# Where the low half of a split weight unit comes from: a VectorE subtraction, or a ScalarE copy and an adding transfer

## The chip, the core and the metric

The kernel runs on one core of a Trainium2 chip. The metric is the device time of one execution in microseconds (us). TensorE (PE) does the matrix products, VectorE (DVE) and ScalarE (ACT) the elementwise work, GpSimd (POOL) a few small operations, and SyncE (SP) issues the loads and stores.

## What is computed

Two layers over 512 tokens of width 1024. Each layer normalises x, projects it to 8192 columns, mixes them by a gated short convolution and by retention over eight heads, and projects back:

```python
for layer in range(DEPTH):                      # DEPTH = 2
    h = rms_norm(x, pre_norm[layer])
    proj = jnp.einsum("bsd,dp->bsp", h, w_in[layer])          # 1024 -> 8192
    ...
    y_conv = c_b * causal_depthwise_conv(c_c * c_x, conv_w[layer])
    y_conv = y_conv * jax.nn.silu(c_z)
    ...
    ret = retention_chunkwise(q, k, v, log_gamma)             # chunks of 128
    ...
    mix = jnp.concatenate([y_conv.astype(h.dtype), y_ret], axis=-1)
    out = jnp.einsum("bse,ed->bsd", mix, w_out[layer])        # 2048 -> 1024
    x = x + rms_norm(out, post_norm[layer]).astype(x.dtype)
```

## The kernel before

The weights stream in as 168 units of 128 partitions x 2 x 512 float32 (512 KB each): 64 of w_in and 24 of w_out in layer 0, then 64 and 16 in layer 1. A unit is a slice of 256 rows of the product's inner dimension. Each product of float32 runs as three passes over operands split in two (hi + lo), so each unit is split once: ScalarE copies it to `wh`, rounded to a shorter significand (line 99), and VectorE subtracts, `wl = raw - wh` (line 100). A unit then feeds 24 matmuls: four targets x two halves x three passes (`mm3`, lines 252 to 254; L252 is hi x hi, and of the other two one takes `wl`).

`raw`, `wh` and `wl` have three buffers each, so unit i takes the buffers of unit i - 3. `prepare` splits units ahead of use, at most to the unit two past the one that PE works on, and `fetch` loads `raw` up to three units past that from SP's queue. So the split of unit i begins when PE has used unit i - 3 for the last time, and has to end before PE comes to unit i.

PE takes the units in groups of four: two together, target by target (`JOINT`), then two singly. A pair of heads takes four such groups, 16 units: the columns v and z (units 0 to 3 of the pair, with the activations as the stationary operand), q and k (4 to 7), and two convolution groups (8 to 11 and 12 to 15), in which the retention's own matmuls stand between the steps. w_out follows each layer. In layer 0 its second half of columns is done in two passes of two targets each, so units 72 to 87 feed only 12 matmuls each; the first units of layer 1 follow right behind.

In a group, the second unit (it takes the buffers of the single unit before) and the fourth (it takes those of the group's first unit) have the shortest time between the release of their buffers and PE's need. Units are counted from 0 here: unit 23 is the last of a q and k group, 25 and 29 are second units of the two convolution groups behind it, 33 the second and 35 the last of the next v and z group.

The framework orders the instructions of each engine by itself; an engine takes its own in order. VectorE also transposes the retention's result (`finish`, line 415), which ScalarE then splits (`mTh<-yT`). GpSimd runs the powers for the norms (lines 231, 396 and 466) and a small memset per convolution (line 427).

Of the kernel before, what the change touches and what calls it, by code (L numbers as in the profile page):

```python
# [12 lines left out]
AF = mybir.ActivationFunctionType  # L13
# [8 lines left out]
NKP = NK // 2  # L22
# [9 lines left out]


def _two_pi_parts():
    """2 * pi in parts (Cody and Waite); n * part is exact for all but the last."""
    rest = 2.0 * np.pi
    parts = []
    for bits in (8, 8, 8):
        e = np.floor(np.log2(abs(rest)))
        q = 2.0 ** (e - bits + 1)  # L40
        part = np.trunc(rest / q) * q
        parts.append(float(part))
        rest -= part
    parts.append(float(np.float32(rest)))
    return parts


# 10000 ** (-i / 64), i < 64, in float32
INV_FREQ = "0000803fd7af5d3f11f93f3fe03d263f9af50f3fcf53f93e9be8d73e1bf8ba3e9be8a13e04358c3e23d4723eed47523e8718363e40b01d3e778d083ed67fec3dcdcccc3d7859b13d0d94993d4dfe843dc255663d3f76473d15ba2c3d4893153de386013dd254e03c4f43c23c8b39a83c39ad913c334d7c3cf27b5a3c11333d3c0ad7233c2de10d3cb0b9f53b15cad43b9c44b83bcc919f3b772e8a3b0e526f3b383e4f3b0f77333b0d691b3b6f94063b2815e93a5cd7c93a8ec9ae3a0e5c973a6f12833ae201633a8c94443a443b2a3a166a133aac4fff392517dd39d774bf3960cba53972928f3915a87839e453573953773a391679213972d40b39e22cf238"

# column offsets in the table of constants
C_INVF = 0
C_MASK = C_INVF + 1
C_ID = C_MASK + P
# [20 lines left out]

@with_exitstack
def hybrid_trunk(ctx: ExitStack, tc, x, x_t, positions, pre_g, post_g, w_in, w_out, conv_w, consts, out):
    """Two layers on one core.

    Every product of a weight runs as three float32r passes over operands split  # L80
    exactly in two (hi + lo). The projection takes h without its factor
    r = rsqrt(mean(x^2) + eps) per token; r is applied behind it. The decays of the
    retention and r are scales of v and of the eps of the head norm.
    """
    nc = tc.nc
    PSUM = bass.MemoryType.PSUM

# [7 lines left out]
    aux = ctx.enter_context(tc.tile_pool(name="aux", bufs=3, space=PSUM))  # L95

    def split(dst_h, dst_l, src):
        """dst_h + dst_l = src, each of 12 significant bits."""
        nc.scalar.activation(out=dst_h, in_=src, func=AF.Copy)  # L99
        nc.vector.tensor_tensor(out=dst_l, in0=src, in1=dst_h.bitcast(F32), op=ALU.subtract)  # L100

# [3 lines left out]
            out=dst_l, in0=src, scalar=scale, in1=dst_h.bitcast(F32), op0=ALU.mult, op1=ALU.subtract  # L105
        )

# [1 line left out]
    units = []  # L109
    for l in range(DEPTH):  # L110
        units += [w_in[l, g, kp] for g in range(NG) for kp in range(NKP)]
# [17 lines left out]
    def prepare(n):  # L129
        while len(ws) <= min(n, len(units) - 1):  # L130
            i = len(ws)
            fetch(i)
            wh = wpool.tile([P, 2, 512], F32R, name=f"wh{i}", tag="wh")
            wl = wpool.tile([P, 2, 512], F32R, name=f"wl{i}", tag="wl")
            if i < NKP:
                for kk in range(2):
                    k = 2 * i + kk
                    split_scaled(hTh0[:, k, :], hTl0[:, k, :], xTs[i][:, kk, :], pre_c[:, 0, k : k + 1])
                    if i == 0:
                        split(wh[:, kk, :], wl[:, kk, :], raws[i][:, kk, :])  # L140
            if i:
                split(wh, wl, raws[i])
            ws[i] = (wh, wl)
            fetch(i + 3)

# [1 line left out]
    warm = cpool.tile([P, 1], F32, name="warm")  # L147
    nc.vector.memset(warm, 0.0)
    nc.scalar.activation(out=warm, in_=warm, func=AF.Silu)
# [5 lines left out]
    hTl0 = hpool.tile([P, NK, SEQ], F32R, name="hTl0", tag="hTl")  # L155
    fetch(2)

    # keeps TensorE's clock up until the first operands are there
    zero = tpool.tile([P, D], BF16, name="zero", tag="junk")
    nc.vector.memset(zero[:, :512], 0.0)  # L160
    pz = aux.tile([P, 512], F32, name="pz", tag="aux")
# [28 lines left out]
    def rotary_tables():  # L190
        ang = tpool.tile([P, SEQ], F32, name="ang", tag="sz")
        nn = tpool.tile([P, SEQ], F32, name="nn", tag="acc")
        nc.vector.tensor_copy(out=nn, in_=pos_i)
        nc.vector.tensor_scalar(
            out=ang, in0=nn, scalar1=cst[:, C_INVF : C_INVF + 1], scalar2=None, op0=ALU.mult
        )
        big = 1.5 * 2.0**23
        nc.vector.tensor_scalar(
            out=nn, in0=ang, scalar1=float(1.0 / (2.0 * np.pi)), scalar2=big, op0=ALU.mult, op1=ALU.add
        )  # L200
        nc.vector.tensor_scalar(out=nn, in0=nn, scalar1=big, scalar2=None, op0=ALU.subtract)
        for part in _two_pi_parts():
            nc.vector.scalar_tensor_tensor(
                out=ang, in0=nn, scalar=-part, in1=ang, op0=ALU.mult, op1=ALU.add
            )
        pi = 3.1415925
        nc.vector.tensor_scalar(out=ang, in0=ang, scalar1=pi, scalar2=-pi, op0=ALU.min, op1=ALU.max)
        nc.scalar.activation(out=sin_t, in_=ang, func=AF.Sin)
        # cos(r) = sin(pi/2 - |r|)
        nc.scalar.activation(out=ang, in_=ang, func=AF.Abs)  # L210
        nc.vector.tensor_scalar(
            out=ang, in0=ang, scalar1=-1.0, scalar2=float(np.pi / 2), op0=ALU.mult, op1=ALU.add
        )
        nc.scalar.activation(out=cos_t, in_=ang, func=AF.Sin)

# [1 line left out]
    def square_sum(l, t):  # L217
        junk = tpool.tile([P, D], BF16, name=f"jx_{l}_{t}", tag="junk", bufs=1)
        sq = nc.scalar.activation(out=junk, in_=xt[t], func=AF.Square, accum_out=sx[l][:, t : t + 1])  # L219
# [1 line left out]
            tc.keep_in_program_order(sq)  # L221

    def token_factors(l):
        """r, v's scale and the head norm's eps, for all tokens."""
        vx = rpool.tile([P, NT], F32, name=f"vx{l}", tag="vx", bufs=1)
        rx = rpool.tile([P, NT], F32, name=f"rx{l}", tag="rx", bufs=1)
        r2 = rpool.tile([P, NT], F32, name=f"r2{l}", tag="r2", bufs=1)
        vt = rpool.tile([P, NT, HEADS], F32, name=f"vt{l}", tag="vt", bufs=1)
        et = rpool.tile([P, NT, HEADS], F32, name=f"et{l}", tag="et", bufs=1)
        nc.vector.tensor_scalar(out=vx, in0=sx[l], scalar1=1.0 / D, scalar2=EPS, op0=ALU.mult, op1=ALU.add)  # L230
        nc.gpsimd.tensor_tensor(out=rx, in0=vx, in1=mhalf[:, :NT], op=ALU.pow)
        nc.vector.tensor_tensor(out=r2, in0=rx, in1=rx, op=ALU.mult)
        nc.vector.tensor_tensor(out=vt, in0=vtab, in1=r2.unsqueeze(2).to_broadcast([P, NT, HEADS]), op=ALU.mult)
        nc.vector.tensor_tensor(out=et, in0=etab, in1=vx.unsqueeze(2).to_broadcast([P, NT, HEADS]), op=ALU.mult)
        return rx, vt, et

    def factor_rows(l, rx):
        """r and r^2 of the tokens along the free dimension, on every partition."""
        rb = tpool.tile([P, NT, P], F32, name=f"rb{l}", tag="u", bufs=1, padded_shape=[P, NT, P + 1])
        nc.vector.tensor_copy(out=rb, in_=rx.unsqueeze(2).to_broadcast([P, NT, P]))  # L240
        ps = aux.tile([P, SEQ], F32, name=f"psr{l}", tag="aux")
# [5 lines left out]
        nc.scalar.activation(out=row2, in_=ps, func=AF.Square)  # L247
        return row, row2

# [1 line left out]
    def mm3(ps, ah, al, bh, bl, first, last):  # L251
        nc.tensor.matmul(out=ps, lhsT=ah, rhs=bh, start=first, stop=False)  # L252
        nc.tensor.matmul(out=ps, lhsT=ah, rhs=bl, start=False, stop=False)  # L253
# [2 lines left out]
    cursor = [0]  # L256

    def run_units(steps, targets, operands, hooks=None):
        """ps[t] += sum over the units. A step names units and targets (None: all) and takes
        the units target by target; hooks[i] are traced behind step i."""  # L260
        base = cursor[0]
        n = 1 + max(u for us, _ in steps for u in us)
        ps = {t: mm.tile([P, 512], F32, name=f"mm{base}_{t}", tag="mm") for t in targets}
# [27 lines left out]
            return wh[:, s], wl[:, s], ah[:, k, :], al[:, k, :]  # L291
        return operands

# [1 line left out]
    def take_vz(l, p, ps, rx, vt):  # L295
        vs, zs = [], []
        for t in range(NT):
# [29 lines left out]
    class Retention:  # L327
# [18 lines left out]
            self.sT.append(s)  # L346

        def k_natural(self, a):
            """Columns 32a : 32a + 32 of k, tokens on partitions."""
            if a == 0:  # L350
                self.kn = rpool.tile([P, 2, NT - 1, P], F32, name=f"kn_{self.tag}", tag="kn", bufs=1)
            src = self.kT.rearrange("p h (t j) -> p h t j", j=P)
            rows = slice(32 * a, 32 * a + 32)
            for b in range(4):
                cols = slice(32 * b, 32 * b + 32)
                nc.vector.transpose(out=self.kn[cols, :, :, rows], in_=src[rows, :, : NT - 1, cols])  # L356
# [49 lines left out]
                    )  # L406

        def finish(self, a):
            """Columns 32a : 32a + 32 of y, transposed; with the last of them, its parts."""
            if a == 0:  # L410
                self.yT = rpool.tile([P, 2, NT, P], F32, name=f"yT_{self.tag}", tag="yT", bufs=1)
            rows = slice(32 * a, 32 * a + 32)
# [4 lines left out]
                e = slice(4 * self.p, 4 * self.p + 2)  # L417
                split(self.mTh[:, e, :], self.mTl[:, e, :], self.yT.rearrange("p h t d -> p h (t d)"))

# [1 line left out]
    def conv(l, ct, ps, row, row2, mTh, mTl):  # L421
        pc, px, pz, pb = ps
        cc = tpool.tile([P, SEQ], F32, name=f"cc_{l}_{ct}", tag="cc")
# [20 lines left out]
        e = 4 * (ct // 2) + 2 + ct % 2  # L444
        split(mTh[:, e, :], mTl[:, e, :], acc)

# [1 line left out]
    def first_half(l, t, ps, og, post):  # L448
        """Columns 0 : 512 of an output row times the gain, and their part of its mean square + eps."""
        ss = rpool.tile([P, 1], F32, name=f"s0_{l}_{t}", tag="s0", bufs=4)  # L450
        v0 = rpool.tile([P, 1], F32, name=f"v0_{l}_{t}", tag="v0", bufs=4)
        junk = tpool.tile([P, 512], BF16, name=f"j0_{l}_{t}", tag="junk", padded_shape=[P, D])
# [34 lines left out]
            split(hTh[:, ks, s], hTl[:, ks, s], xg)  # L487
        return emit

# [1 line left out]
    hTh, hTl = hTh0, hTl0  # L491
    fac = {}

# [88 lines left out]


def _packed(x, positions, pre_norm, w_in, conv_w, w_out, post_norm):
    """The inputs laid out as the kernel reads them."""
    col = lambda kind, i: np.arange(kind * 1024 + i * P, kind * 1024 + (i + 1) * P)
    groups = []
    for p in range(NPAIR):
# [49 lines left out]
```

## Time and profile before

| | |
|---|---|
| time, median of 3 runs | 942.76 us (942.73 to 943.03) |
| profiled execution: span from the first to the last instruction | 941.0 us |
| median less that span | 1.8 us |
| PE busy | 933.1 us, 99% |
| DVE busy | 596.7 us, 63% |
| ACT busy | 278.4 us, 30% |
| POOL busy | 24.6 us, 3% |
| mean DMA rate | 103 GB/s |

The busy time of an engine is that of its instructions, waits left out. Matmuls overlap one another in the records, so a busy PE says that it had work, not that it ran at its peak. The timed runs carry no profile of their own; the profile is of one execution with the span above.

### The profile page before, as it was taken

To read this page: it belongs to the slowest core of one execution; us is meant where nothing else is said; L and a number is where in the kernel's file an instruction comes from. 1 tells how busy PE (TensorE), PEld (TensorE's weight loads), DVE (VectorE), ACT (ScalarE), POOL (GpSimd) and SP (SyncE) were. 2 spreads that over 40 slices of the span, in tenths; PEclk is the share of its full clock that TensorE was granted. 3 is DMA by queue.
4 is the path that set the end of the run, shared out by engine and by line. 5 is a ranking of instruction groups with operands and counts; after the bars stand their busy time and mean duration, and the time that the engine had idled before them with its cause. 6 is when DMAs were issued, how large, how long until landed. Compare 5 with 4: busy or idle time off the path is not lost.

```text
span 941.0 us, 10986 instructions
## 1 busy us (share of the span) xinstructions
PE 933.1 (99%) x4338; PEld 776.0 (82%) x4338; DVE 596.7 (63%) x960; ACT 278.4 (30%) x450; POOL 24.6 (3%) x46
## 2 busy tenths in 40 slices
PE   9999999999999999999999999999999999999997
PEld 6788888888888888888888888888888888888886
DVE  5595839583958395825764948394849484947324
ACT  5522331222133213324542133213321332222311
POOL 0000000000000000000000000000000000000000
PEclk9999999999999999999999999999999999999999
DMA  8522132213222322235532222322222222222222
GB/s 309 178 92 90 53 127 90 90 63 116 90 90 68 112 90 90 71 108 179 178 122 103 91 90 79 100 90 90 88 92 90 90 90 90 90 91 90 89 68 90
DMA packets 27700, 96.60 MB, mean 103 GB/s; under 512 B 3328, under 2 KB 3456, under 8 KB 27648
## 3 DMA queue, kind: packets, MB, share of 16 engines
q1 hardware_dynamic: 27504, 95.88, 30.7%
q8 instruction: 34, 0.56, 0.2%
q14 instruction: 18, 0.15, 0.1%
q10 hardware_dynamic: 144, 0.01, 0.0%
HBM read 93.78 MB, written 2.10 MB: 102 GB/s over the span
## 4 chain that ended last, share of the span: by engine, by line
PE 94%; DMA 2%; DVE 1%; ACT 1%; issue 1%; POOL 0%; SPq 0%; DVEq 0%; POOLq 0%; ACTq 0%
PE mm L252 30%; PE mm L254 29%; PE mm L253 29%; PE pa L378 2%; PE pss L339 2%; PE pa L382 1%; PE pk L361 1%; DMA xT<-in_x_t 1%; DMA x<-in_x 1%; DVE wl L100 1%; DMA pre_c<-in_pre_norm 0%; DVE x L470 0%; PE psx L481 0%; ACT wh L99 0%; ACT jx L219 0%
## 5 line engine op out<-in xcount | busy, mean ns | idle before, releaser
L100 DVE TENSOR_TENSOR wl<-raw,wh 128x1024 fp32r<-128x1024 f32 (+1 forms) x169 | 205.4, 1217 | 226.5 <-ACT wh L99 222.8
L99 ACT ACTIVATE wh<-raw 128x1024 fp32r<-128x1024 f32 (+1 forms) x169 | 178.1, 1054 | 470.6 <-PE mm L253 303.1
L252 PE MATMUL mm<-hTh,wh 128*128 128x512 f32 x768 | 302.5, 394 | 0.1
L254 PE MATMUL mm<-hTh,wl 128*128 128x512 f32 x768 | 299.8, 390 | 0.3 <-DVE wl L100 0.3
L253 PE MATMUL mm<-hTl,wh 128*128 128x512 f32 x768 | 298.7, 389 | 0.0
L254 PEld LDWEIGHTS mm<-hTh,wl 128*128 128x128 f32 x768 | 144.1, 188 | 31.4 <-DVE wl L100 0.7
L252 PEld LDWEIGHTS mm<-hTh,wh 128*128 128x128 f32 x768 | 144.3, 188 | 29.3 <-ACT z L304 0.6
L253 PEld LDWEIGHTS mm<-hTl,wh 128*128 128x128 f32 x768 | 144.3, 188 | 29.1
L252 PE MATMUL mm<-wh,hTh 128*128 128x512 f32 x256 | 99.6, 392 | 0.3 <-ACT hTh L99 0.3
L253 PE MATMUL mm<-wl,hTh 128*128 128x512 f32 x256 | 99.8, 390 | 0.0
L254 PE MATMUL mm<-wh,hTl 128*128 128x512 f32 x256 | 99.8, 390 | 0.0
L252 PE MATMUL mm<-wh,mTh 128*128 128x512 f32 x256 | 99.8, 390 | 0.0
L254 PE MATMUL mm<-wh,mTl 128*128 128x512 f32 x256 | 99.6, 389 | 0.0
L253 PE MATMUL mm<-wl,mTh 128*128 128x512 f32 x256 | 99.6, 389 | 0.0
L252 PEld LDWEIGHTS mm<-wh,hTh 128*128 128x128 f32 x256 | 48.1, 189 | 11.5 <-ACT wh L99 1.2
L415 DVE STREAM_TRANSPOSE yT<-y 32x256 f32<-32x256 f32 x128 | 55.8, 436 | 2.1
L253 PEld LDWEIGHTS mm<-wl,hTh 128*128 128x128 f32 x256 | 48.1, 188 | 10.5 <-DVE wl L100 0.6
L254 PEld LDWEIGHTS mm<-wh,mTl 128*128 128x128 f32 x256 | 48.0, 188 | 10.1
L254 PEld LDWEIGHTS mm<-wh,hTl 128*128 128x128 f32 x256 | 48.1, 188 | 9.9
L252 PEld LDWEIGHTS mm<-wh,mTh 128*128 128x128 f32 x256 | 48.1, 188 | 9.9
L253 PEld LDWEIGHTS mm<-wl,mTh 128*128 128x128 f32 x256 | 48.1, 188 | 9.9
L356 DVE STREAM_TRANSPOSE kn<-qk 32x192 f32<-32x192 f32 x128 | 47.3, 370 | 2.0
(85 smaller groups left out, 596.3 us busy)
## 6 DMA issues: line engine op xcount, KB each, us to landing
raw<-in_w_in SPq DMA_DIRECT2D x127, 512.0 KB, 3.3
raw<-in_w_out SPq DMA_DIRECT2D x40, 512.0 KB, 3.3
x<-in_x SPq DMA_DIRECT2D x4, 512.0 KB, 7.2
out<-x SPq DMA_DIRECT2D x8, 256.0 KB, 2.1
xT<-in_x_t SPq DMA_DIRECT2D x3, 512.0 KB, 7.7
post<-in_post_norm SPq DMA_DIRECT2D x2, 512.0 KB, 5.5
xT<-in_x_t SPq DMA_DIRECT2D x2, 256.0 KB, 3.9
raw<-in_w_in SPq DMA_DIRECT2D x2, 256.0 KB, 4.2
```

Source lines behind the costliest of these rows:

```text
L99: nc.scalar.activation(out=dst_h, in_=src, func=AF.Copy)
L100: nc.vector.tensor_tensor(out=dst_l, in0=src, in1=dst_h.bitcast(F32), op=ALU.subtract)
L252: nc.tensor.matmul(out=ps, lhsT=ah, rhs=bh, start=first, stop=False)
L253: nc.tensor.matmul(out=ps, lhsT=ah, rhs=bl, start=False, stop=False)
L254: nc.tensor.matmul(out=ps, lhsT=al, rhs=bh, start=False, stop=last)
L339: nc.tensor.matmul(out=pss[:, j, :], lhsT=self.kT[:, h, s], rhs=self.qT[:, h, s], start=True, stop=True)
L356: nc.vector.transpose(out=self.kn[cols, :, :, rows], in_=src[rows, :, : NT - 1, cols])
L361: nc.tensor.matmul(out=pk[:, h, :], lhsT=self.kn[:, h, t, :], rhs=self.vs[t][:, h, :], start=True, stop=True)
L378: nc.tensor.matmul(out=pa[:, j, :], lhsT=self.sT[b][:, j, :], rhs=self.vs[t][:, h, :], start=True, stop=(t == 0))
L382: nc.tensor.matmul(out=pa[:, j, :], lhsT=self.qT[:, h, t * P : (t + 1) * P], rhs=self.S[t][:, h, :], start=False, stop=True,)
L415: nc.vector.transpose(out=self.yT[rows, :, :, cols], in_=self.y[cols, :, :, rows])
```

## The change

For units 4 to 167, ScalarE writes `wl = -wh`: the copy of the raw unit with the scale -1, rounded as `wh` is. A transfer issued from GpSimd's queue then reads the unit from HBM a second time and adds it to what lies in `wl`. ScalarE makes `wh` by its own copy of `raw`. Units 0 to 3 are split as before. The activations' own splits (`mTl`, `hTl`) stay with VectorE. The change also drops comments, which moves line numbers by up to five.

```diff
@@ prepare(n), where unit i is split @@
-            if i:
+            if 0 < i < NKP:
                 split(wh, wl, raws[i])
+            elif i:
+
+                nc.scalar.activation(out=wl, in_=raws[i], func=AF.Copy, scale=-1.0)
+                nc.gpsimd.dma_start(out=wl, in_=units[i], accum_op=ALU.add)
+                nc.scalar.activation(out=wh, in_=raws[i], func=AF.Copy)
             ws[i] = (wh, wl)
             fetch(i + 3)
```

On ScalarE, at the end of a v and z group (units 34 and 35, then 36 and 37 of the q and k group; `mTh<-acc` and `mTh<-yT` split the mixers' results), the order before is:

```order
L99 ACTIVATE wh34_1544<-raw34_1422 128x1024
L99 ACTIVATE mTh0_156<-acc_0_3_1553 128x512
L99 ACTIVATE wh35_1620<-raw35_1428 128x1024
L99 ACTIVATE mTh0_156<-yT_0_1_1632 128x1024
L99 ACTIVATE wh36_1626<-raw36_1490 128x1024
L99 ACTIVATE wh37_1665<-raw37_1548 128x1024
```

The same place on ScalarE with the change:

```order
L145 ACTIVATE wl34_1575<-raw34_1450 128x1024
L147 ACTIVATE wh34_1574<-raw34_1450 128x1024
L99 ACTIVATE mTh0_156<-acc_0_3_1584 128x512
L99 ACTIVATE mTh0_156<-yT_0_1_1665 128x1024
L145 ACTIVATE wl35_1652<-raw35_1457 128x1024
L147 ACTIVATE wh35_1651<-raw35_1457 128x1024
L145 ACTIVATE wl36_1659<-raw36_1520 128x1024
L147 ACTIVATE wh36_1658<-raw36_1520 128x1024
```

Each unit has two copies now, and both copies of unit 35 have moved behind `mTh<-yT`, the split of the transposed retention result.

On ScalarE at the change from the q and k group (units 20 to 23) to the first convolution group (24 to 27), the order with the change is the following; before, one `wh` copy per unit stood there, in the order 23, 24, 25, 26, 27.

```order
L147 ACTIVATE wh23_1114<-raw23_963 128x1024
L145 ACTIVATE wl23_1115<-raw23_963 128x1024
L145 ACTIVATE wl24_1122<-raw24_1003 128x1024
L147 ACTIVATE wh24_1121<-raw24_1003 128x1024
L147 ACTIVATE wh25_1152<-raw25_1044 128x1024
L145 ACTIVATE wl25_1153<-raw25_1044 128x1024
```

Although the source writes `wl` first, the framework puts `wh` first for units 23 and 25 (and likewise for 27, 29, 31 and 33 and for the same units of the other pairs); `wl` is the second copy there.

On GpSimd's queue before, at the end of the same pair of heads (`ra` the powers of the head norm, `u` the memsets of the convolutions):

```order
L396 TENSOR_TENSOR ra_0_1_0_1454<-va_0_1_0_1453,mhalf_150 128x4
L396 TENSOR_TENSOR ra_0_1_1_1513<-va_0_1_1_1512,mhalf_150 128x4
L427 MEMSET u_0_4_2033 128x2
L427 MEMSET u_0_5_2235 128x2
L396 TENSOR_TENSOR ra_0_2_0_2138<-va_0_2_0_2137,mhalf_150 128x4
```

With the change, from the same `ra` on:

```order
L401 TENSOR_TENSOR ra_0_1_0_1483<-va_0_1_0_1482,mhalf_150 128x4
L146 DMA wl33_1516<-in_w_in 128x1024
L401 TENSOR_TENSOR ra_0_1_1_1543<-va_0_1_1_1542,mhalf_150 128x4
L146 DMA wl34_1575<-in_w_in 128x1024
L432 MEMSET u_0_4_2076 128x2
L146 DMA wl35_1652<-in_w_in 128x1024
L146 DMA wl36_1659<-in_w_in 128x1024
L146 DMA wl37_1699<-in_w_in 128x1024
```

The adding transfers, 164 in all, now stand between the powers and the memsets, and each waits in the queue for its copy by ScalarE.

## Rows read from the trace of the kernel before

**Rows 1.** The page: span, and busy time of each engine

```profile
span 941.0 us, 10986 instructions
...
PE 933.1 (99%) x4338; PEld 776.0 (82%) x4338; DVE 596.7 (63%) x960; ACT 278.4 (30%) x450; POOL 24.6 (3%) x46
```

**Rows 2.** The page: chain that ended last, shares of the span by engine

```profile
PE 94%; DMA 2%; DVE 1%; ACT 1%; issue 1%; POOL 0%; SPq 0%; DVEq 0%; POOLq 0%; ACTq 0%
```

**Rows 3.** Waits of PE: us in total, times, longest

```profile
PE mm L252 <- ACT hTh L99: 0.3, 1, 0.3
PE mm L254 <- DVE wl L100: 0.3, 1, 0.3
```

**Rows 4.** Groups by line and form: busy us, mean ns; idle before

```profile
L100 DVE TENSOR_TENSOR wl<-raw,wh 128x1024 fp32r<-128x1024 f32 x167 | 204.1, 1223 | 226.5 <-ACT wh L99 222.8
L99 ACT ACTIVATE wh<-raw 128x1024 fp32r<-128x1024 f32 x167 | 176.8, 1059 | 470.6 <-PE mm L253 303.1 <-PE mm L254 99.4 <-issue 66.0
```

**Rows 5.** Transfers: queue of the loads, raw units, all raws' time to landing

```profile
q1 hardware_dynamic: 27504, 95.88, 30.7%
...
raw<-in_w_in SPq DMA_DIRECT2D x127, 512.0 KB, 3.3
...
DMA to landing us min/median/max: 3.1/3.3/8.4
```

**Rows 6.** ACT in order of time: start us, us, instruction [idle before]

```profile
132.78 1.06 ACT L99 ACTIVATE wh<-raw 128x1024 fp32r<-128x1024 f32 x1 [7.87 <-issue]
...
162.23 1.06 ACT L99 ACTIVATE wh<-raw 128x1024 fp32r<-128x1024 f32 x1 [5.33 <-PE mm L253]
...
187.23 1.06 ACT L99 ACTIVATE wh<-raw 128x1024 fp32r<-128x1024 f32 x1 [3.69 <-PE mm L253]
...
204.70 1.06 ACT L99 ACTIVATE wh<-raw 128x1024 fp32r<-128x1024 f32 x1 [2.61 <-PE mm L254]
208.04 1.07 ACT L99 ACTIVATE mTh<-yT 128x1024 fp32r<-128x1024 f32 x1 [2.28 <-DVE yT L415]
```

**Rows 7.** PE in order of time: first matmuls on wl of units 23, 29, 33, 35

```profile
140.01 0.39 PE L254 MATMUL mm<-hTh,wl 128*128 128x512 f32 x1
...
170.46 0.39 PE L254 MATMUL mm<-hTh,wl 128*128 128x512 f32 x1
...
196.57 0.39 PE L253 MATMUL mm<-wl,hTh 128*128 128x512 f32 x1
...
211.53 0.39 PE L253 MATMUL mm<-wl,hTh 128*128 128x512 f32 x1
```

**Rows 8.** DVE in order of time, ahead of mTh<-yT at 208.04

```profile
197.18 1.20 DVE L100 TENSOR_TENSOR wl<-raw,wh 128x1024 fp32r<-128x1024 f32 x1
198.32 0.73 DVE L438 SCALAR_TENSOR_TENSOR acc<-u,cw,acc 128x512 f32<-128x512 f32 x1
...
203.51 4.50 DVE L415 STREAM_TRANSPOSE yT<-y 32x256 f32<-32x256 f32 x10
```

**Rows 9.** Groups on POOL: busy us, mean ns

```profile
L396 POOL TENSOR_TENSOR ra<-va,mhalf 128x4 f32<-128x4 f32 x16 | 16.2, 1010 | 169.4 <-DVE va L392 169.4
```

**Rows 10.** Unit 6: its copy on ACT, and PE's first matmul on its wl

```profile
28.46 1.05 ACT L99 ACTIVATE wh<-raw 128x1024 fp32r<-128x1024 f32 x1
...
31.86 0.50 PE L254 MATMUL mm<-hTh,wl 128*128 128x512 f32 x1 [0.27 <-DVE wl L100]
```

**Rows 11.** PE: first matmuls on units 75 and 77 (two targets each)

```profile
433.67 0.39 PE L252 MATMUL mm<-wh,mTh 128*128 128x512 f32 x1
...
439.11 0.39 PE L252 MATMUL mm<-wh,mTh 128*128 128x512 f32 x1
```

**Rows 12.** Stretch of units 72 to 87: us, busy times, PEclk, DMA share, GB/s

```profile
425.50:470.80 45.30, 45.30 (x209) 37.68 (x208) 29.71 (x38) 23.89 (x32) 1.65 (x3) 1.00 0.55 175
```

**Rows 13.** First and last stretch, the same columns

```profile
0.00:2.00 2.00, 0.78 (x2) 0.28 (x3) 0.35 (x3) 0.83 (x1) 0.20 (x4) 1.00 0.11 13
...
935.00:941.00 6.00, 0.03 (x1) 0.00 (x0) 2.64 (x5) 0.69 (x2) 0.54 (x1) 0.74 0.47 175
```

## The prediction, made before the change was run

> **What bounds the kernel now.** I read the page first. PE is busy for 933.1 of 941.0 us, VectorE for 63% and ScalarE for 30% [rows 1], and the chain that ended last runs over PE for 94% [rows 2]. The view of the waits, taken for PE alone, then shows that PE waited for the split of a unit or of the activations for 0.6 us in the whole span [rows 3]. So the split is hidden completely: taking work from VectorE can give back 0.6 us at most, and anything that brings a `wl` late is paid in full. The question is therefore how long the new way to `wl` takes, and how much time each unit has for it.
>
> **What is removed and added.** VectorE loses 164 subtractions of 1.223 us [rows 4], 201 us of busy time that nobody waited for; it should fall to some 396 us. ScalarE gains 164 copies; its present copy of the same shape takes 1.059 us [rows 4], so 174 us more and some 452 busy, 48%. As a load that is harmless; in the chain of one unit it counts. Before, a `wl` was ready one copy and one subtraction after the buffer's release, 1.06 + 1.22 us. Now it is ready after one copy (two where `wh` stands first) and a transfer. SP gets its `raw` buffer back after two copies instead of a copy and a subtraction, 2.12 against 2.28 us: no change. On GpSimd's queue a transfer waits for its copy, and behind it wait the powers and the memset; VectorE waits for the powers. Both stand where their inputs are long ready: the memset ahead of unit 35's transfer waits for VectorE's convolution step at 198.32 [rows 8], before that unit's copy starts. I cost it at nothing; uncovered, a power is 1.01 us [rows 9].
>
> **The price of an adding transfer, D,** from its issue to landed. The trace has none, so I bound it. A plain load of a unit takes 3.3 us (3.1 the fastest, 8.4 the slowest) [rows 5]. The load queue moved 95.88 MB in 30.7% of 16 engines' 941.0 us, which is 1.58 us of all 16 engines per 0.524 MB; the remaining 1.7 us of the 3.3 is not moving. Low end: as a plain load, 3.3 us. High end: the slowest load and 1.0 us of work on GpSimd, the nearest row there being a power [rows 9]: 9.4 us. My value lies between: the transfer reads both the unit and what lies in `wl`, twice the bytes, so 1.7 + 2 x 1.58, plus 1.0 on GpSimd, plus half of the plain load of `raw` (0.8) that SP issues at the same moment onto the same engines: **6.7 us**.
>
> The Trainium skill bears on this twice. Its page "DMA: Bandwidth & Descriptors" (Anatomy of one DMA) gives a transfer from GpSimd 2.0 us and its bytes at 436 GB/s, 3.2 us for a unit, and "Collectives: The Full Stack" (The bandwidth ceiling) says that an adding transfer runs at half the rate of a copy because it reads two sources. By the two pages an estimate of D is 4.4 us, and the sum below would be 43 us instead of 84.
>
> **The time that each unit has.** I take one pair of heads, units 23 to 37, and set the start of ScalarE's copy [rows 6] against PE's first matmul on that `wl` [rows 7]. Unit 23: 132.78 to 140.01, 7.23 us. Unit 29: 162.23 to 170.46, 8.23. Unit 33: 187.23 to 196.57, 9.34. Unit 35: 204.70 to 211.53, 6.83. These are the short ones; at each border of two groups the last unit of the one and the second of the next are both short, but a wait for the first moves PE's need for the second too, so each border is paid once. Units in other places have 8 us and more, the shortest of them right behind the wait for unit 35.
>
> - Border of the q and k group to the first convolution: both copies come first, so 2.12 + 6.7 = 8.8 against 7.23: 1.6 us, eight times (four pairs, two layers): 13 us.
> - First to second convolution: 8.8 against 8.23: 0.6 us, eight times: 5 us.
> - Second convolution to v and z (or w_out): 8.8 against 9.34: nothing. Here retention's matmuls are the cover.
> - End of v and z: both copies of unit 35 now stand behind `mTh<-yT`, which waited until VectorE's last transpose at 208.01 [rows 6, 8]. One 1.20 us subtraction ahead of the transposes [rows 8] goes, so it runs from 206.8 to 207.9, the copy ends at 208.96, `wl` lands at 215.7 against a need at 211.53: 4.1 us. Six such ends and two in w_out: 33 us. This is the dearest place, and a queue order makes it.
> - Three more borders without that obstacle (at the starts of w_out's second half, of layer 1, and of the last half), with `wl` first: 1.06 + 6.7 = 7.8 against 6.83: 3 us.
> - Unit 6: 28.46 + 1.06 + 6.7 = 36.2 against 31.86 [rows 10]: 4 us, once.
> - Units 72 to 87: PE takes 2.72 us per unit [rows 11]. The engines moved data for 55% of 45.3 us [rows 12], 1.56 us per unit, so the raw loads alone fill half of that time. With the adding transfers it is 1.58 + 3.16 = 4.74 us per unit, 76 us for 16 units. PE's 45.3 us and the three raw units loaded ahead (4.7) cover the rest: 26 us. The buffers turn over three units in 7.8 + 2.7 us, 3.5 per unit, so the transfers and not the latency bind here.
>
> Sum: 13 + 5 + 33 + 3 + 4 + 26 = 84 us. Against its own span, 941.0 + 84 = 1025; the timed median stands 1.8 us over the span, so **1027 us**.
>
> The same sum at the ends. D = 3.3: only unit 35's kind (208.96 + 3.3 - 211.53 = 0.7, eight times) and unit 6 (1.0) remain, and the 16 units cost 51 - 45.3 - 4.7 = 1: 8 us in all, **951 us**. D = 9.4: 34 + 26 + 17 (now 2.2 us at the third border too) + 55 + 11 + 7, and 26 for the 16 units: 176 us, **1119 us**.
>
> **The rivals.**
>
> *Not slower.* The transfer is hidden anyway, about 943 us. It is decided at unit 35: with D below 211.53 - 208.96 = 2.6 us nothing waits there, and everywhere else more time is left. Against it: the fastest plain load took 3.1 us, and an adding one cannot well be quicker. A gain is nearly excluded, since PE has 0.6 us to get back.
>
> *A cheap transfer.* D near that of a plain load, 951 to 985 us (3.3 to 4.4 us). For it: the engines are at 30% over the span, and they could read the two sources side by side. Most of the loss would then lie at the ends of v and z.
>
> *The transfers become the bound everywhere.* If one adding transfer takes the engines more than 4 us, the 168 units no longer fit the mean of 5.6 us per unit (941.0 / 168) beside the raw load. At four times a plain load, 1.58 + 6.3 = 7.9 us per unit, 164 units take 1296 us, and with the first 28 us, before unit 4 is needed, the time is about 1325. Nothing in the trace speaks for a factor of four; nothing shows an adding transfer either.
>
> *PE's clock.* The granted clock held through the first 1.2 us without work, but in the last 6 us, after PE's last matmul, its mean is 0.74 [rows 13], so it fell to 1.2 GHz within them. Waits of 4 us at eight places could lower it. The price is a bound: one 5.44 us unit (twice the 2.72) at half speed after each, 8 x 5.4 = 43 us on top, 1070 us. The Trainium skill's "TensorE: Matmul & The Clock Gate" (HAM oscillation) describes just this, an engine that waits for transfers and starts its next stretch cold; the 0.74 agrees that it can happen, no wait in mid-kernel here shows it.
>
> **How the numbers follow.** D from 4.4 to 8.5 us, 985 to 1090 us: 0.50 with the forecast in it and, of that, 0.12 for the clock's case. The cheap transfer: 0.20. D above that, up to 1180 us: 0.12. The engines as the bound, over 1180: 0.13. Hidden: 0.05. A kernel of this kind can be told from no change at about 0.2%, 2 us. Faster than that gets 0.02 and no change 0.03, both out of the hidden case; slower 0.95. The range from 955 to 1180 us leaves out the engine-bound case and the hidden one, just under 2 in 10.
>
> **What the profile after would show.** VectorE near 396 us busy and ScalarE near 452; HBM reads up by 164 units of 0.524 MB, 86 MB. PE with waits for the transfers into `wl`, some eight of about 4 us at the ends of v and z, waits of one or two us at the q and k borders, none at the third border, and a denser patch in the 16 half units. The issue-to-landing column gives D itself. The prediction is wrong if D is far from 6.7 us, if GpSimd issues late because a power or a memset stands ahead, if the DMA share stays near 1.0 outside the 16 units, or if the granted clock is well below 1.00 behind the waits.

## The result, and the profile after

The changed kernel takes **1103.39 us**, the median of four executions, against 942.75 us for the kernel before in the same comparison. One of the four, on which the first profile fell, ran at a mean granted clock of 0.653 and took 1363.34 us, so the ratio of 1.169 (95% interval 1.166 to 1.172) and the 159 us by which the kernel is slower go by the other three (median 1101.35 us), and the rows of after below come from the same kernel run once more (e1, 1101.14 us). The forecast was 1027 us, with 955 to 1180 us as its range.

> The changed kernel once more, for a profile at a granted clock like that of its quick timed executions (0.97). If the waits for the adding transfers are the cause, PE shows some 120 to 160 us of waits for wl transfers, most at the ends of v and z groups (about 5 us each), at the q and k borders (about 3) and in the 16 half units, with a time from issue to landing of 7 to 8 us. If the clock is the cause, PE's waits are below 60 us and the matmuls' spacing is longer than 0.227 us for long stretches.

The page of that run, with span, busy times, the two transfer queues (q0 carries the adding transfers, q1 SP's loads), HBM and the chain:

```profile
span 1099.4 us, 11287 instructions
...
PE 981.8 (89%) x4338; PEld 790.6 (72%) x4338; DVE 406.9 (37%) x796; ACT 429.4 (39%) x614; POOL 167.9 (15%) x210
...
q0 software_dynamic: 23616, 85.99, 43.8%
q1 hardware_dynamic: 27504, 95.88, 25.7%
...
HBM read 179.77 MB, written 2.10 MB: 165 GB/s over the span
...
issue 42%; DMA 28%; PE 20%; POOL 4%; DVE 4%; ACT 2%; SPq 0%; POOLq 0%; DVEq 0%; ACTq 0%
```

VectorE fell from 596.7 to 406.9 us [rows 1], as forecast, and it is worth nothing. PE, which had been 99% busy, is at 89%, and the chain that ran over PE for 94% [rows 2] now runs over it for 20%. PE's waits (us in total, times, longest) stand beside the 0.6 us of [rows 3]:

```profile
PE mm L259 <- DMA wl<-in_w_in: 47.4, 27, 5.3
PE mm L258 <- DMA wl<-in_w_in: 32.2, 14, 3.9
PE mm L258 <- DMA wl<-in_w_out: 27.8, 19, 3.5
```

That is 107.4 us in 60 waits, all for the adding transfers. The rest is in PE's own busy time, 981.8 against 933.1 us for the same 4338 matmuls: 48.7 us more. Together these are 156 of the 158 us by which the span grew. So the waits are fewer than the 120 to 160 us expected of e1, and more than the 60 us under which the clock alone would have been the cause.

Not all of the 48.7 us is the clock's. The mean granted clock fell from 0.998 to 0.968, and 0.030 of 1099.4 us is 33 us at most. The rest fits the overlap that each wait breaks: matmuls start every 0.227 us and last 0.39 us each, and at a wait the last and the first of them stand alone. In e2 below, where the clock's mean is 0.997 and PE waits 17 times for a transfer, PE is still busy for 940.8 us, 7.7 more than before.

The transfer itself, in the view of the tile `wl` (from issue to landed):

```profile
DMA to landing us min/median/max: 5.3/8.1/11.9
```

The median is 8.1 us where I had put 6.7. Followed unit by unit in PE's order of time, the waits fall where the prediction had looked for them. At the q and k borders: 25 us (13 forecast). First to second convolution: 16.5 us (5). Second convolution to v and z or w_out: 6.8 us (nothing). Ends of v and z: 28.0 us, eight times 3.1 to 3.9 (33). The other borders: 6.2 us (3). Units 5 and 6: 6.0 us (4). The half units and unit 89 behind them: 19 us (26).

Unit 35 again, in ScalarE's, GpSimd's, SP's and PE's order of time (start us, us, instruction, [idle before <- releaser]):

```profile
240.73 1.06 ACT L99 ACTIVATE mTh<-yT 128x1024 fp32r<-128x1024 f32 x1 [5.50 <-DVE yT L420]
241.69 1.04 ACT L145 ACTIVATE wl<-raw 128x1024 fp32r<-128x1024 f32 x1
242.64 1.04 ACT L147 ACTIVATE wh<-raw 128x1024 fp32r<-128x1024 f32 x1
...
243.03 0.86 POOL L146 DMA_DIRECT2D wl<-in_w_in  x1 [10.63 <-ACT wl L145]
...
243.71 4.61 SPq L127 DMA_DIRECT2D raw<-in_w_in  x3
...
250.06 0.79 PE L258 MATMUL mm<-wl,hTh 128*128 128x512 f32 x1 [3.67 <-DMA wl<-in_w_in]
250.65 0.63 PE L259 MATMUL mm<-wh,hTl 128*128 128x512 f32 x1
```

The copy into `wl` stands behind `mTh<-yT`; the transfer starts on GpSimd at 243.03; and at 243.71, as soon as the second copy has released the `raw` buffer, SP's next loads go onto the same engines. PE waits 3.67 us. Behind the wait its matmuls last 0.63 us, not 0.39 [rows 7]. The windows there (busy times of PE, its weight loads, DVE, ACT and POOL, then PEclk, DMA share, GB/s) say why:

```profile
246.00:250.00 4.00, 0.39 (x2) 0.00 (x0) 0.00 (x0) 1.97 (x2) 0.86 (x1) 0.99 1.03 258
250.00:252.00 2.00, 1.95 (x5) 1.56 (x6) 0.00 (x0) 0.00 (x0) 0.00 (x0) 0.50 1.02 266
252.00:254.00 2.00, 2.00 (x8) 1.58 (x7) 0.42 (x1) 0.47 (x1) 0.00 (x0) 0.66 1.04 272
254.00:256.00 2.00, 2.00 (x10) 1.67 (x9) 0.66 (x2) 0.47 (x1) 0.00 (x0) 1.00 1.06 283
```

While PE waits the DMA engines are full (share 1.03). Then the granted clock is 0.50, the lower level of 1.2 GHz, for two us, and is back at 1.00 four us after the wait. Over the span its mean is 0.968.

### The profile page after: what moved, and what is told of

The parts are those of the page before. It is cut to its first block, busy times and chain, and to the rows that moved or that the text cites. A ratio compares the mean times of both kernels' runs of the same rounds, so it can differ in the third digit from the quotient of the medians.

```text
span 1361.5 us, 11287 instructions
## 1 busy us (share of the span) xinstructions
PE 1343.0 (99%) x4338; PEld 877.5 (64%) x4338; DVE 409.4 (30%) x796; ACT 434.4 (32%) x614; POOL 167.8 (12%) x210
## 3 DMA queue, kind: packets, MB, share of 16 engines
q1 hardware_dynamic: 27504, 95.88, 21.0%
## 4 chain that ended last, share of the span: by engine, by line
PE 86%; issue 9%; DMA 3%; POOL 1%; ACT 1%; DVE 0%; POOLq 0%; DVEq 0%; ACTq 0%
PE mm L258 27%; PE mm L259 27%; PE mm L257 27%; DMA wl<-in_w_out 2%; PE pss L344 2%; PE pa L383 1%; PE pk L366 1%; DMA wl<-in_w_in 1%; PE pa L387 1%; POOL wl L146 1%; ACT wl L145 0%; DMA pre_c<-in_pre_norm 0%; DVE ang L208 0%; ACT wh L147 0%; POOL r L471 0%
## 5 line engine op out<-in xcount | busy, mean ns | idle before, releaser
L257 PE MATMUL mm<-hTh,wh 128*128 128x512 f32 x768 | 394.4, 514 | 0.1
L259 PE MATMUL mm<-hTh,wl 128*128 128x512 f32 x768 | 390.3, 508 | 3.5 <-DMA wl<-in_w_in 3.5
L258 PE MATMUL mm<-hTl,wh 128*128 128x512 f32 x768 | 390.0, 508 | 0.0
L147 ACT ACTIVATE wh<-raw 128x1024 fp32r<-128x1024 f32 x164 | 171.9, 1048 | 496.8 <-issue 362.0
L145 ACT ACTIVATE wl<-raw 128x1024 fp32r<-128x1024 f32 x164 | 172.6, 1052 | 206.1 <-PE mm L258 195.6
L146 POOL DMA_DIRECT2D wl<-in_w_in x124 | 108.0, 871 | 827.4 <-ACT wl L145 813.4
L258 PE MATMUL mm<-wl,mTh 128*128 128x512 f32 x256 | 130.1, 508 | 4.5 <-DMA wl<-in_w_out 4.3
L259 PE MATMUL mm<-wh,hTl 128*128 128x512 f32 x256 | 130.5, 510 | 0.0
L259 PE MATMUL mm<-wh,mTl 128*128 128x512 f32 x256 | 130.3, 509 | 0.0
L257 PE MATMUL mm<-wh,mTh 128*128 128x512 f32 x256 | 129.9, 509 | 0.0
```

The costliest lines, as they stand in the source:

```text
L145: nc.scalar.activation(out=wl, in_=raws[i], func=AF.Copy, scale=-1.0)
L146: nc.gpsimd.dma_start(out=wl, in_=units[i], accum_op=ALU.add)
L147: nc.scalar.activation(out=wh, in_=raws[i], func=AF.Copy)
L259: nc.tensor.matmul(out=ps, lhsT=al, rhs=bh, start=False, stop=last)
```

## The experiments

Theory A: PE waits where a unit has less time than a transfer takes, and the transfer takes 8.1 us because it shares the engines with the `raw` load that is released at the same moment. Theory B: the adding transfers cost by themselves, whatever the order and the sharing. Theory C: PE's fallen clock is a cost of its own, some 49 us.

**e2: only even units by the adding transfer**

```diff
-            if 0 < i < NKP:
+            if 0 < i < NKP or i % 2:
```

> Only the even units from 4 on are made by the copy and the adding transfer; odd units (second and last of each group, the ones with the short time) are split by ScalarE and VectorE as before. If the loss lies in the short times of the odd units, 945 to 960 us, since the even units have 10 us and more and the engines have room in the half units (1.6 + 1.5 us per 2.7). If adding transfers cost by themselves (engines, GpSimd, clock), half of the loss stays: about 1020 us.

989.92 us, ratio 1.050 (1.045 to 1.055). It fell between the two expectations: half of the transfers cost 47 us, not 159, and PE waited 31.4 us. Those waits stand in unit 6, in units 20, 36, 52 and their like (1.6 to 2.5 us, the units right behind `mTh<-yT`), and in the even half units. So even units are not all safe; e10 keeps those without a wait.

**e3: the retention's `finish` one step later**

```diff
-                hooks = {i: [lambda r=done, a=a: r.finish(a) for a in (2 * i, 2 * i + 1)] for i in range(2)}
+                hooks = {i + 1: [lambda r=done, a=a: r.finish(a) for a in (2 * i, 2 * i + 1)] for i in range(2)}
```

> The transposes of retention's result, and with them ScalarE's mTh<-yT, are placed one step later, behind the third unit of a v and z group. If the queue order on ScalarE is worth 4 to 5 us at eight places, about 25 us less than the changed kernel (1075 us), as the wait at unit 35 shrinks from 5 to 2 us. If the wait is only passed on to the copies of units 36 and 37, or the order is not the cause, within 10 us of 1101.

1109.81 us, ratio 1.171 (1.164 to 1.178). This tells nothing on the order, since the edit did not change it: the framework put `mTh<-yT` ahead of the copies again, as ScalarE's rows show:

```profile
243.51 1.06 ACT L99 ACTIVATE mTh<-yT 128x1024 fp32r<-128x1024 f32 x1 [5.50 <-DVE yT L420]
244.48 1.05 ACT L145 ACTIVATE wl<-raw 128x1024 fp32r<-128x1024 f32 x1
```

**e4: units 72 to 89 by VectorE**

```diff
-            if 0 < i < NKP:
+            if 0 < i < NKP or 72 <= i < 90:
```

> Units 72 to 89 are split by ScalarE and VectorE as before, all others by the adding transfer. If the transfers fill the engines in the half units, 26 to 40 us less than the changed kernel: 1060 to 1075. If the half units lose nothing of their own, 1095 to 1105.

1075.03 us, ratio 1.141 (1.136 to 1.146): 26 us less than e1, the size of the prediction's term.

**e5: the same transfer without the addition**

```diff
-                nc.gpsimd.dma_start(out=wl, in_=units[i], accum_op=ALU.add)
+                nc.gpsimd.dma_start(out=wl, in_=units[i])
```

The kernel then leaves out the subtraction: `wl` holds the raw weights.

> The transfer from GpSimd's queue copies the raw unit over wl and adds nothing (the output lacks the subtraction: wl holds the raw weights). ScalarE's two copies, the queue, the bytes fetched and every wait stay. If the adding is what makes the transfer long (8.1 us from issue to landing, 2.94 us of 16 engines in the changed kernel), it should land in 4.5 to 6 us and take about 1.5 us of the engines, the waits of TensorE fall from 107 us to 20 to 45 us and the time to 970 to 1010 us. If the way by GpSimd's queue and the sharing with the raw loads make it long, whatever the transfer does, it stays at 1085 to 1105 us.

980.82 us, ratio 1.040 (1.038 to 1.043). The page's line of the queue:

```profile
q0 software_dynamic: 23616, 85.99, 27.1%
```

and the landing, in the view of the tile:

```profile
DMA to landing us min/median/max: 3.4/4.5/9.0
```

27.1% of 979.8 us over 164 transfers is 1.62 us of the 16 engines for a copy; 43.8% of 1099.4 us is 2.94 us for an adding transfer. The same queue, the same number of issues and the same bytes fetched, less the addition, leave 38 of 159 us. (GpSimd's time per issue falls too, from 0.86 to 0.53 us.)

**e6: the adding transfer's source in SBUF**

```diff
-                nc.gpsimd.dma_start(out=wl, in_=units[i], accum_op=ALU.add)
+                nc.gpsimd.dma_start(out=wl, in_=raws[i], accum_op=ALU.add)
```

> The adding transfer reads the raw unit from its buffer in SBUF, not a second time from HBM. If the second read from HBM sets the length of the transfer, it lands 1.5 us or more sooner and the time is 1010 to 1060 us. If the adding itself sets it (read, add and write of the target), landing stays at 7 to 9 us and the time at 1085 to 1110 us, with HBM reads back near 94 MB.

1032.93 us, ratio 1.095 (1.093 to 1.097). At first sight this is the second read from HBM. The rows say otherwise. The page's line of the queue, and the tile's view:

```profile
q0 software_dynamic: 23616, 85.99, 46.8%
...
DMA to landing us min/median/max: 4.5/5.6/10.4
```

and GpSimd, SP and PE in order of time at unit 35:

```profile
229.98 0.86 POOL L146 DMA_DIRECT2D wl<-raw  x1 [10.63 <-ACT wl L145]
...
234.59 3.18 SPq L127 DMA_DIRECT2D raw<-in_w_in  x2
...
234.58 0.50 PE L258 MATMUL mm<-wl,hTh 128*128 128x512 f32 x1 [2.29 <-DMA wl<-raw]
```

The engines' time per transfer is unchanged (46.8% of 1030.2 us over 164: 2.94 us). But the transfer now holds the `raw` buffer until it has landed, so SP's next load starts at 234.59, the moment PE gets its `wl`, and not beside it. The wait for unit 35 is 2.29 us in place of 3.67. The read itself counts for little: with no load beside it, unit 35's transfer landed in 4.55 us from SBUF and in 5.09 us from HBM (e7, next), half a microsecond, against the 2.5 us by which the median fell.

**e7: no `raw` loads beside the transfers**

```diff
             i = len(raws)
+            if i >= 6:
+                raws[i] = raws[3 + i % 3]
+                continue
```

The copies then read a stale unit, so `wh` and `wl` are another split of the unit than the true one.

> Units 6 to 167 have no raw load: their two copies on ScalarE read three buffers loaded once (so hi is of the wrong weights, and the output is not the trunk's). The adding transfers stay, alone on the engines. If the raw load beside it is what stretched an adding transfer from my 6.7 to 8.1 us, it lands in 5 to 6.5 us, the waits fall by 1.5 to 3 us at each of some 50 places and the time is 980 to 1035 us. If the adding transfers wait for one another or for GpSimd, landing stays above 7 us and the time above 1080 us.

1006.97 us, ratio 1.067 (1.064 to 1.070). The tile's view:

```profile
DMA to landing us min/median/max: 5.0/5.2/10.2
```

The engines' time per transfer is again 2.95 us (48.2% of 1004.6 us over 164).

So without the `raw` loads an adding transfer lands in 5.2 us, with the source in HBM as before. The sharing is 2.9 us of the 8.1, and 94 of the 159 us. (The loads share HBM with it as well as the engines; no run takes the two apart.) PE's waits for the transfers are 36.0 us here:

```profile
PE mm L261 <- DMA wl<-in_w_in: 20.1, 8, 3.0
PE mm L261 <- DMA wl<-in_w_out: 12.0, 9, 2.9
PE mm L262 <- DMA wl<-in_w_in: 3.9, 3, 2.2
```

**e8: matmuls of zeros in place of the waits**

```diff
                     wh, wl = ws[base + u]
+                    for _ in range(FILL.get(base + u, 0) if t == (ts or targets)[0] else 0):
+                        nc.tensor.matmul(out=ps[t], lhsT=zf, rhs=zf.unsqueeze(1).to_broadcast([P, 4, P]),
+                                         start=False, stop=False)
```

> Ahead of 17 units behind which the granted clock of TensorE fell in the changed kernel (or whose wait was about 3 us) TensorE does 7 to 20 matmuls of zeros into the open accumulator, about as long as the wait was; nothing else changes, so the wait turns into work of the same length. If the longer busy time of TensorE (982 us against 933 us) comes from the clock that falls behind a wait of 3 us, the clock stays at 1.00 there and the time is 1065 to 1085 us. If it has another cause (contention with the transfers, say), it stays at 1098 to 1110 us.

1099.58 us, ratio 1.166 (1.161 to 1.172): no gain. Yet the clock held at 15 of the 17 places (not behind units 7 and 87); around unit 35 the windows read

```profile
255.00:257.00 2.00, 1.15 (x5) 0.58 (x4) 0.00 (x0) 0.00 (x0) 0.00 (x0) 1.00 1.00 254
257.00:259.00 2.00, 2.00 (x10) 1.61 (x9) 0.42 (x1) 0.37 (x1) 0.00 (x0) 1.00 1.05 276
```

PE's group of the zeros (busy us, mean ns):

```profile
L278 PE MATMUL mm<-zf 128*128 128x512 bf16 x218 | 52.2, 390 | 0.0
```

and its waits:

```profile
PE mm L261 <- DMA wl<-in_w_in: 45.8, 32, 5.0
PE mm L260 <- DMA wl<-in_w_out: 20.3, 19, 2.8
PE mm L260 <- DMA wl<-in_w_in: 9.9, 12, 1.8
```

Without the zeros PE is busy for 1015.6 - 52.2 = 963.4 us, 18.4 less than in e1. Waits and zeros together are 76.0 + 52.2 = 128.2 us, 20.8 more than the waits of e1. But three blocks of zeros stood where no wait was:

```profile
41.74 6.40 PE L278 MATMUL mm<-zf 128*128 128x512 bf16 x20
...
67.69 0.79 PE L261 MATMUL mm<-hTh,wl 128*128 128x512 f32 x1 [5.04 <-DMA wl<-in_w_in]
...
579.24 2.12 PE L278 MATMUL mm<-zf 128*128 128x512 bf16 x9
...
584.84 2.12 PE L278 MATMUL mm<-zf 128*128 128x512 bf16 x9
```

The 20 zeros meant for unit 7 ran 21 us before its wait began, and the wait stayed; unit 89 is taken in three steps and got its nine zeros at each, twice in vain. These blocks are 10.6 of the 20.8 us. Only 6.7 us went into longer waits at units without zeros (58.8 us in place of 52.1), unit 127 above all (3.44 us in place of 1.06). So e8 is no clean test: it doesn't show what holding the clock is worth in the full kernel, and theory C stays open here.

**e9: `mTh<-yT` behind three more units' copies**

`finish` leaves the split of `yT` to a call `finish(4)` in `hooks[2]`, for six of the eight groups, and keeps it there:

```diff
+                hi = nc.scalar.activation(out=self.mTh[:, e, :], in_=src, func=AF.Copy)
+                if a == 4:
+                    tc.keep_in_program_order(hi)
```

> In six of the eight v and z groups the copy mTh<-yT now stands behind wl36, wl37 and wl38 on ScalarE (the edit of e3 had left the order as it was), so wl35 and its like start as soon as their buffer is free, about 2.5 us sooner. If the place behind mTh<-yT makes those waits, they fall from 3.1 to 3.8 us to below 1.5 us at six places and the time to 1075 to 1092 us. If the transfers of the neighbouring units limit that stretch anyway, the wait moves to the next units and the time stays at 1095 to 1107 us.

1089.37 us, ratio 1.154 (1.148 to 1.160), some 12 us better. Now the copy of unit 35 waits for its buffer only, and PE:

```profile
236.46 1.06 ACT L145 ACTIVATE wl<-raw 128x1024 fp32r<-128x1024 f32 x1 [3.64 <-PE mm L258]
...
244.74 0.50 PE L258 MATMUL mm<-wl,hTh 128*128 128x512 f32 x1 [1.06 <-DMA wl<-in_w_in]
...
271.53 0.50 PE L259 MATMUL mm<-hTh,wl 128*128 128x512 f32 x1 [3.39 <-DMA wl<-in_w_in]
```

At the six places the waits fell from 21 to 6.4 us, which confirms the order as the cause of that part. In all PE's waits fell by 10.9 us only (96.5 against 107.4): later units wait longer, unit 39 (271.53) 3.39 us in place of 3.07, unit 55 3.26 in place of 2.27.

**e10: only units whose time is long enough**

```diff
-            if 0 < i < NKP:
+            if 0 < i < NKP or i not in HIDDEN:
...
+HIDDEN = [i for i in range(8, 168, 2) if i % 16 != (4 if i < 88 else 12) and not 72 <= i < 90]
```

> Only 62 units go by the adding transfer: even ones that are neither behind mTh<-yT nor among units 72 to 89; all others keep VectorE. If a transfer costs time only where wl is wanted less than some 8 us after its buffer is free, all 62 are hidden and the time is 943 to 948 us. If adding transfers cost by themselves (the memory they share with TensorE's reads, GpSimd's issues, the engines), it is 955 to 985 us.

948.62 us, ratio 1.006 (1.004 to 1.008), at the upper end of what was expected if all are hidden. The landing is 7.6 us at the median for the 52 units of w_in, and PE waits for none of the 62. Beside 1.2 us for a memset, as before, PE's only wait is in the start-up, where no adding transfer has been issued yet:

```profile
PE mm L258 <- ACT wh L100: 3.8, 1, 3.8
```

The window of the first 20 us there (busy times, PEclk, DMA share, GB/s):

```profile
0.00:20.00 20.00, 14.93 (x44) 9.93 (x45) 11.43 (x17) 11.82 (x16) 0.20 (x4) 0.83 0.78 288
```

In its first 20 us PE ran 44 matmuls (70 before); at 0.227 us each (24 of them between the two rows of [rows 11], 5.44 us) the missing 26 are 5.9 of the 6.5 us by which the span is longer (947.5 against 941.0). PE comes to unit 1 5.9 us later than before and to the last unit 5.9 us later, so in sum nothing is lost in between. In the start-up ScalarE has a copy of `wh` ahead of an `hTh` in another order than before; why that costs 3.8 us was not tested. The 62 transfers by themselves cost nothing that shows.

**e11 and e12: e7 with zeros at the eight ends of v and z; e7 with e9's order**

The diffs are those of e7 and e8 (10 matmuls for each of units 19, 35, 51, 67, 107, 123, 139, 155), and of e7 and e9.

> As e7 (no raw load for units 6 to 167), with 10 matmuls of zeros ahead of each of the eight units behind mTh<-yT, about 2.3 us of their 2.9 us wait. If TensorE's fallen clock adds to the time where the units behind a wait have their weights in time, the clock stays at 1.00 there and the time falls from 1007 to 988 to 998 us. If slow TensorE work only takes the place of waits, as the result of e8 suggests, it stays at 1003 to 1012 us.

> e7 and e9 together. If the order on ScalarE makes the waits at the ends of the v and z groups, six of the eight waits of 2.9 us fall below 1 us and, with the slow clock behind them, the time from 1007 to 975 to 992 us. If not, 1000 to 1010 us.

e11: 996.65 us, ratio 1.057 (1.055 to 1.058). e12: 978.42 us, ratio 1.038 (1.035 to 1.041). With the `raw` loads gone, few units behind these waits wait in their turn, and both effects show: holding the clock gives 10 us (in e11 the windows around unit 35 are at 1.00 throughout, and waits and zeros together are as long as e7's waits), and the order 29 us for six places, against 12 us in e9. PE's waits in e12:

```profile
PE mm L261 <- DMA wl<-in_w_out: 11.5, 8, 3.2
PE mm L262 <- DMA wl<-in_w_in: 4.6, 4, 2.5
PE mm L261 <- DMA wl<-in_w_in: 2.7, 2, 1.7
```

So 17 of the 29 us are waits (two of the eight remain, those in w_out, at 2.89 and 3.15 us) and 9 are PE's busy time (947.7 against 956.4 us), in which the mean clock rose from 0.983 to 0.991.

## Why the prediction was right in sign and short in size

- **What bounds it, and that nothing is to gain:** right. 190 us less on VectorE gave nothing back, and of PE's new waits 107.4 us are for `wl`, some 1 us for `wh`.
- **The time that each unit has:** right, and the best part of it. Put the measured 8.1 us into its formulas and the q and k borders give 2.12 + 8.1 - 7.23 = 3.0 us, eight times 24 (25 measured); the convolution borders 16 (16.5); the third border 7 (6.8); the other three borders 7 (6.2); unit 6 gives 6 (6.0, with unit 5's). Only the ends of v and z come out too long, 44 against 28: PE's need came 3.66 us behind the copy's end (242.73 to 246.39, the end of the last matmul ahead), not 2.57, and that transfer landed 7.0 us from its issue, not 8.1.
- **D:** the step that failed. "Half of the plain load of `raw` (0.8)" was mis-sized; it is 2.9 us (8.1 with the loads, 5.2 without, e7). One load beside the transfer is worth 1.9 us (unit 35: 6.98 us in e1, 5.09 in e7), more than the load's own 1.55 us of the engines (25.7% of 1099.4 us, times 0.524 of 95.88 MB) and not half of it. The rest comes from the next units' transfers, each with a load of its own: unit 36's, issued 1.9 us later, landed in 9.05 us (5.80 in e7), and unit 37's in 11.32 (6.62). The other terms were near: 6.7 - 0.8 = 5.9 forecast against 5.2; 3.16 us of the engines against 2.94; GpSimd 0.87 us per issue against 1.0. Of the Trainium skill's two pages, "DMA: Bandwidth & Descriptors" (Anatomy of one DMA) and "Collectives: The Full Stack" (The bandwidth ceiling), the second agrees in kind: adding took 2.94 us of the engines against 1.62, nearly half the rate. The estimate of 4.4 us from both was 0.8 below the transfer alone, and it counts no sharing.
- **The waits:** 84 us forecast, 107 measured. With D at 8.1 us the formulas give 130; the ends of v and z (44 against 28) and the half units (26 against 19) take back what they give too much.
- **The number:** D was 8.1 us, within the case of 4.4 to 8.5 us, but the time of 1101 us lies above the 985 to 1090 us of that case, in the bracket that was kept for a longer D (0.12). That the range held it is in part luck: PE's longer busy time was not in the sum.
- **The clock:** I had it as a rival, at most 43 us. It happened: "TensorE: Matmul & The Clock Gate" (HAM oscillation) in the Trainium skill describes it, and the 0.50 behind the wait for unit 35 agrees. PE's busy time grew by 48.7 us, of which the clock is 33 us at most. What holding it would give back in the full kernel stays open, since e8 is no clean test; without the `raw` loads it is some 10 us for eight places (e11). The error was to hold "forecast" and "forecast with the clock" apart as two cases, where waits of that length make it the likeliest one.
- **The half units:** 26 us forecast; 26 by e4, of which 19 are waits.
- **GpSimd's powers and memset at nothing:** right. In e1 162 of the 164 transfers were issued within 0.4 us of the end of their copy; the other two (units 64 and 117, 0.96 and 2.25 us) have no power or memset as their releaser in the trace, and PE waited for neither.
- **Rivals:** "hidden" fell (but holds for the 62 units of e10). "Cheap transfer" fell: even a plain copy on that way costs 38 us (e5). The engines as the bound everywhere fell: e7 and e10 show time behind most units.

So theory A holds. C holds in kind, since the clock falls behind the waits and costs time (e11), but at less than its 49 us. B holds only in that the addition makes the transfer long, not that it costs where there is time.

## What to carry to other kernels

Before a step is moved from a compute engine to a transfer, set the transfer's full latency against the shortest time between the release of a buffer and its use, place by place; an idle-looking engine and an idle-looking queue say nothing of it. Ask what else the same release starts: here the copies that fed the transfer also freed the buffer for the next load, and the two shared the engines every time. Where TensorE waits for chained transfers, later waits can take back part of what a cure gives: in e9 the six places lost 14.7 us of waits, and all places together 10.9.

## What had not been expected of the hardware

- An adding transfer of 512 KB from GpSimd's queue took 2.94 us of the 16 engines wherever its source lay (SBUF or HBM), against 1.62 us without the addition, and 5.2 us from issue to landing (source in HBM) with no load beside it.
- The clock did not fall behind every long wait. Unit 23 had waited 3.03 us, and the windows behind it stay at 1.00; unit 39 had waited 3.07 us, and there the clock fell. The two, in that order:

```profile
169.00:171.00 2.00, 1.43 (x6) 1.21 (x7) 0.20 (x1) 0.00 (x0) 0.11 (x1) 1.00 1.02 277
171.00:173.00 2.00, 2.00 (x10) 1.64 (x10) 1.94 (x4) 0.00 (x0) 0.00 (x0) 1.00 1.01 328
...
277.00:279.00 2.00, 1.97 (x5) 1.58 (x6) 0.01 (x1) 0.00 (x0) 0.00 (x0) 0.56 1.03 315
279.00:281.00 2.00, 2.00 (x6) 1.55 (x6) 1.97 (x3) 0.00 (x0) 0.00 (x0) 0.58 1.05 274
```

So a wait's length alone does not tell whether slow matmuls follow it; what else decides it stays open here.
